# Six staging tiles for the outputs of a down projection, packed operands, and the order of two weight loads in a decoder step

## The chip, the core and the metric

The kernel runs on one core of a Trainium2 chip. The metric is the device time of one execution in microseconds (us); lower is better. The kernel's median over 3 runs is 1246.54 us (1244.26 to 1247.14). Line numbers (L303) are those of the kernel before, unless a row is said to be of the changed one, where most lines are one less or more.

## The reference

One step of a decoder layer for 512 prompt tokens and 8 x 4 sample tokens (544 columns in all), D_MODEL 1024, D_FF 2816. Two token mixers (a gated convolution and a sparse attention) are merged, then comes the part that the change works on:

```
x  = x + g1 * (merged @ w_out)
h2 = rmsnorm(x, norm2) * (1 + sc2) + sh2
x  = x + g2 * ((silu(h2 @ w_gate) * (h2 @ w_up)) @ w_down)
y  = rmsnorm(x, norm_f)
```

All of it is fp32.

## The kernel before

**Arithmetic.** Every fp32 operand is split into a high and a low part (`to_hilo`: ACT rounds the high part, L396, DVE subtracts for the low part, L397), and a product is three matmuls (`mm3`): high x high (L254), high x low (L255), low x high (L256), each 128 x 128 by 272 columns in the part spoken of here. Results gather in PSUM.

**The FFN.** The 22 chunks of 128 hidden features are worked in pairs c2 = 1 to 10; chunks 0 and 1 are done ahead, by plain products (the loop over `early`, whose gate tiles `ffg` lie in a pool of their own, `wx`). The hidden dimension is cut into four phases for the down projection, of 4, 6, 6 and 6 chunks. A pair of output tiles is computed by `seven`, a scheme with seven block products in place of eight: `wpair` is a generator that issues the seven products of one pair, `product` their matmuls into the PSUM tiles wA, wB and wC, and `snap` (L303, ACT) copies an intermediate sum of wA into a quarter of the tile `work`. Between them DVE adds a snap to the PSUM tile of the next result and writes the output (`out`). The last two products of a pair (`rest`) are held back and issued in the middle of the next pair. A pair takes a slab of weights (`slab`, L240, requested by SP, from a ring of three buffers `raw`) and, for its block sums, a second, partly summed tile `ws` (L318, SP too, two buffers); DVE completes these by two additions (L359, L364), and ACT and DVE split them.

`combine` makes the sums of the input h2 that the scheme multiplies with: t0 to t3, four `tf` tiles in the pool `f6`, split into T1 to T4 in hooks that run during the first pairs.

**Phases.** Phase 0 is `down_plain`, run during c2 = 2: eight outputs m by plain products. `gated` (ACT L1835, and DVE L1838 for the sample columns) scales the result by g2 from PSUM into a staging tile of 128 x 544, and `add_x1` (L1841) has POOL start a DMA that adds the staging tile onto x in DRAM (`x_dr<-work`, 272 KB). Four staging tiles are used in turn: the two halves of `U` and of `Gs[1]`. Phases 1 and 2 are `down_seven`, run during c2 = 5 and c2 = 8 between the gate and the up product: four pairs dn0 to dn3 of two outputs. `dn_out` adds a snap into the staging tile (DVE L1863), scales it in place, and `add_x1` sends it when its second half is there. The first result of a pair goes to its first tile, the second one to the second tile, `rest` completes the second tile and then the first:

```
for m2, ts in enumerate(((u0, u1), (v0, v1), (u1, u0), (v1, v0))):
```

u0, u1 are the halves of `U`, v0, v1 those of `Gs[ph - 1]`. So dn2 first writes u1, which dn0 completed first. Phase 3 ends the kernel with plain products and the final norm.

**Memory.** `work` holds Gs[0], Gs[1], U and the four snaps; each gate product writes Gs[c2 % 2] (L1767), each up product writes U (L1779, L1814) and multiplies. A tile that is written again waits for its readers, the DMA out to DRAM among them. [...]

Of the kernel before, what the change touches and what calls it, by code (L numbers as in the profile page):

```python
# [10 lines left out]
F32 = mybir.dt.float32  # L11
# [12 lines left out]
NT = TP + TS  # L24
# [134 lines left out]
def build(tc, a, o):  # L159
# [30 lines left out]
    def nm(s):  # L190
        uid[0] += 1
        return f"{s}_{uid[0]}"
# [93 lines left out]
    def seven(o_, ww, wlp, wsp):  # L286
        wi, ns, late = [0], [0], [iter(())]
        hooks = iter(o_.splits)

        def wsplit(view, odd=None):  # L290
            nk = view.shape[1]
            if odd is None:
                wi[0] += 1
                odd = wi[0] % 2
            pools = ((wpool, "wh"), (wpool, "wl")) if odd else ((ww, "Wh"), (wlp, "Wl"))
            wh, wl = (p_.tile([128, 8, 128], F32R, tag=t, bufs=2, name=nm(t))[:, 0:nk, :] for p_, t in pools)
            to_hilo(view, wh, wl)
            return wh, wl

        def snap(p):  # L300
            t = o_.snaps[ns[0] % 4]
            ns[0] += 1
            o_.snap_ops.append(act.activation(t, p, AF.Copy))  # L303
            return t

        def product(p, w, k0, X, first):
            n_ = len(X[0]) if isinstance(X[0], list) else 4
            xk = lambda t, k: t[k] if isinstance(t, list) else t[:, k, :]
            k0 *= n_
            for k in range(n_):  # L310
                mm3(p, w[0][:, k0:k0 + n_], w[1][:, k0:k0 + n_], xk(X[0], k), xk(X[1], k), k, first and k == 0, k == n_ - 1, skip_group_check=not first)

        def wslab(*key):
            raw = slab(*key)
            n_ = len(SLABS[key][1]) // 4
            if key in pre:
                t = wsp.tile([128, 16, 128], F32, tag="ws", bufs=2, name=nm("ws"))
                sync.dma_start(t[:, n_:3 * n_].rearrange("p k f -> p (k f)"), pre[key][:, 0:256 * n_])  # L318
                y, z = t[:, 0:2 * n_], t[:, 2 * n_:4 * n_]
            else:  # L320
                y, z = (wsp.tile([128, 8, 128], F32, tag="ws", bufs=3, name=nm("ws"))[:, 0:2 * n_] for _ in range(2))
            q = raw.rearrange("p k f -> p (k f)").rearrange("p (n k f) -> p n k f", n=4, k=n_)
            return q, y, z, key in pre

        def prepare(slabs):

            raw, y, z, summed = slabs
            n_ = raw.shape[2]
            y1, y2, z1, z2 = y[:, 0:n_], y[:, n_:2 * n_], z[:, 0:n_], z[:, n_:2 * n_]
            a22, a21, a11, a12 = (raw[:, i] for i in range(4))  # L330
            W0 = wsplit(raw[:, 2:4].rearrange("p n k f -> p (n k) f"))
            if not summed:
                dve.tensor_add(y2, a21, a22)
            dve.tensor_add(y1, y2, a11)
            WY = wsplit(y)
            if not summed:
                dve.tensor_add(z1, a11, a21)
            dve.tensor_add(z2, y1, a12)
            return W0, WY

        def wpair(slabs, out, ready=None, o_=o_, tie=None):

            raw, y, z, summed = slabs
            n_ = raw.shape[2]
            y1, y2, z1, z2 = y[:, 0:n_], y[:, n_:2 * n_], z[:, 0:n_], z[:, n_:2 * n_]
            a22, a21, a11, a12 = (raw[:, i] for i in range(4))
            W0 = wsplit(raw[:, 2:4].rearrange("p n k f -> p (n k) f")) if ready is None else ready[0]
            pA = s_ps(nm("wA"))[:, 0:WH]
            product(pA, W0, 0, o_.B11, True)
            s1 = snap(pA)  # L350
            pB = lin_ps(nm("wB"))[:, 0:WH]
            product(pB, W0, 1, o_.B21, True)
            out(0, 0, pB, s1)
            yield
            if ready is None:
                if not summed:
                    dve.tensor_add(y2, a21, a22)
                with tc.issue_after(tie.ins) if tie else ExitStack():
                    dve.tensor_add(y1, y2, a11)  # L359
                WY = wsplit(y)  # L360
                if not summed:
                    dve.tensor_add(z1, a11, a21)
                with tc.issue_after(tie.ins) if tie else ExitStack():
                    dve.tensor_add(z2, y1, a12)  # L364
            else:
                WY = ready[1]
            WZ = wsplit(z)
            W3 = wsplit(a22)
            product(pA, WY, 0, o_.T2, False)
            s2 = snap(pA)  # L370
            next(hooks, lambda: None)()
            pC = lin_ps(nm("wC"))[:, 0:WH]
            product(pC, WY, 1, o_.T1, True)
            next(late[0], None)
            next(hooks, lambda: None)()
            product(pA, WZ, 0, o_.T3, False)
            s3 = snap(pA)
            out(1, 1, pC, s3)
            next(hooks, lambda: None)()

            def rest():
                product(pA, W3, 0, o_.T4, False)
                out(1, 0, pA, None)
                yield
                product(pC, WZ, 1, o_.B22, False)
                out(0, 1, pC, s2)
                yield
            late[0] = rest()
            yield
        return SimpleNamespace(wsplit=wsplit, wslab=wslab, wpair=wpair, late=late, prepare=prepare)  # L390
# [1307 lines left out]
    def combine():  # L1698

        fq = lambda k, q: h2f[:, kq[k], Q[q]]  # L1700
        t0, t1 = (f6_tile(i, [128, 4, WH], F32, "tf") for i in (6, 7))
        t2, t3 = (f6_tile(i, [128, 4, WH], F32, "tf") for i in (3, 2))
        act.activation(t2, fq(0, 1), AF.Copy, scale=-1.0)
        pool.dma_start(t2, fq(1, 1), accum_op=ALU.add)
        dve.tensor_sub(t0, fq(0, 0), fq(0, 1))
        act.activation(t3, fq(1, 0), AF.Copy)
        dve.scalar_tensor_tensor(t1, t0, -1.0, fq(1, 1), ALU.mult, ALU.subtract)
        pool.dma_start(t3, t1, accum_op=ALU.add)
        to_hilo(t1, *T2)

        def split_t3():
            with tc.issue_after(snap_ops[1].ins):
                to_hilo(t2, *T3)

        def split_t4():
            with tc.issue_after(snap_ops[1].ins):
                act.activation(T4[0], t3, AF.Copy, scale=-1.0)
                dve.scalar_tensor_tensor(T4[1], t3, -1.0, T4[0].bitcast(F32), ALU.mult, ALU.subtract)
        return [lambda: to_hilo(t0, *T1), split_t3, split_t4]

    early = []
    wxst = ExitStack()
    wx = mkpool(wxst, "wx", side="right")
    for c in range(2):
        cs = slice(c * 128, c * 128 + 128)
        w = [split(v[:, :, cs]) if c == 0 else tuple(f6_tile(2 + 2 * n_ + j, [128, 8, 128], F32R, "wx") for j in range(2)) for n_, v in enumerate((sg, su))]
        if c:
            with tc.issue_after(n2_ops[0][0].ins), tc.issue_after(n2_ops[0][1].ins):
                to_hilo(sg[:, :, cs], *w[0])
        ffn_tiles(c)  # L1730
        early.append((c, wx.tile([128, NT], F32, name=nm("ffg")), w))
    for hf in range(2):
        for c, g_, w in early[::1 - 2 * hf]:
            ffn_gate(g_, w[0], hf)
# [6 lines left out]
                    to_hilo(su[:, :, 128:256], *early[1][2][1])  # L1741
        if hf == 0:
            ops_.splits = combine()
    wxst.close()
    n2st.close()
    work = wk.tile([128, KC * NT], F32, tag="work", bufs=1, name="work")
    cut = lambda i, n: work[:, i * WH:(i + n) * WH]
# [44 lines left out]
    def up_seven(G, c2):  # L1792
        if c2 % 3 == 2:
            tt = [f_x[:, 4 * i:4 * i + 4] for i in range(2)]
            bb = [f_x[:, 8 + i] for i in range(6)]
        else:
            tiles = [f6_tile(4 * (c2 % 3 == 0) + i, [128, 4, WH], F32R, "fs") for i in range(4)]
            tt = tiles[0:2]
            bb = [tiles[2 + i // 4][:, i % 4] for i in range(6)]
        ops = fops.setdefault((c2 - 2) // 3, {n: ([], []) for n in ("B11", "B21", "B22", "T1", "T2", "T3", "T4")})  # L1800
        for n, i in (("B11", 0), ("B21", 2), ("B22", 4)):
            for x in range(2):
# [40 lines left out]
    def down_plain():  # L1843

        nk = PHASES[0][1]
        stg = [t[:, m, :] for t in (U, Gs[1]) for m in range(2)]
        for m in range(KC):
            if m % 2 == 0:
                sl_ = slab("dn", 0, m // 2)
            w = split(sl_[:, :, (m % 2) * 128:(m % 2) * 128 + 128], nk=nk)  # L1850
            t = stg[m % 4]
            for hf in range(2):
                p = lin_ps(nm("dn"))[:, 0:HW[hf]]
                for k in range(nk):
# [14 lines left out]

    def down_seven(ph):  # L1870
        o_ = SimpleNamespace(**fops[ph - 1])
        u0, u1, v0, v1 = (t[:, m, :] for t in (U, Gs[ph - 1]) for m in range(2))
        for m2, ts in enumerate(((u0, u1), (v0, v1), (u1, u0), (v1, v0))):
            yield wslab("dn", ph, m2), dn_out(m2, ts), o_

    def finish_pair():
# [193 lines left out]
```

## Time and profile before

| | |
|---|---|
| median of 3 runs | 1246.54 us |
| the profiled execution | 1244.05 us, its span 1242.3 us |
| mean granted TensorE clock | 0.994 |
| PE busy, of the 840 us up to the FFN's pairs | 828.56 us |
| PE busy, of the 402.3 us after that | 380.73 us |
| copies of staging tiles to DRAM | 24, of 272 KB, median 7.5 us to landing |

A row of the timeline has the start, the length, the engine and line, the operation, what it writes and reads, and in brackets the idle time of the engine just before and what ended it. Rows of the stretches give length, busy time (and count) for PE, PE's weight loads, DVE, ACT and POOL, the granted clock (1.00 is full), the share of the DMA engines, and GB/s.

### The profile page before, as it was taken

Reading aid. Unit: us, or ns where it says so; the run is one execution under the profiler, and the core shown is the slowest. Engines: PE = TensorE matmul, PEld = TensorE weight load, DVE = VectorE, ACT = ScalarE, POOL = GpSimd, SP = SyncE. Lnnn points to the kernel's source line nnn. Section 1 sums busy time; section 2 is a strip of 40 time slices with the busy share of each in tenths; the row PEclk is TensorE's granted clock in tenths of the full one; section 3 lists DMA queues with packets and bytes.
Section 4 is the critical chain, followed back from the end, with each engine's and each line's share of the span. In section 5 each row is a group of like instructions: output and inputs, shape, how many; then the busy total and the mean of one; then the engine's idle time right before and its main releaser. Section 6 shows DMA issues by size and latency. Waiting matters only on the chain.

```text
span 1242.3 us, 25810 instructions
## 1 busy us (share of the span) xinstructions
PE 1209.3 (97%) x10158; PEld 1113.3 (90%) x10158; DVE 845.0 (68%) x1891; ACT 673.5 (54%) x1323; POOL 100.1 (8%) x154
## 2 busy tenths in 40 slices
PE   8999999999999999999999999999999998998997
PEld 6998999999999888787777779999899998998997
DVE  4467646887775576686776866758747856876766
ACT  5556535664445333386766664437555655665542
POOL 1000210000000111120100100000020011001000
PEclk9999999999999999999999999999999999999999
DMA  8953238787674998979787878716385366447612
GB/s 283 407 201 139 90 131 215 234 247 215 206 207 150 367 329 299 313 211 247 212 232 213 235 225 267 269 64 175 109 224 171 119 188 205 151 138 213 205 52 73
DMA packets 83660, 255.65 MB, mean 206 GB/s; under 512 B 9160, under 2 KB 19272, under 8 KB 69338
## 3 DMA queue, kind: packets, MB, share of 16 engines
q1 hardware_dynamic: 70994, 230.51, 53.3%
q0 software_dynamic: 12112, 23.09, 11.4%
q8 instruction: 80, 1.31, 0.4%
q10 hardware_dynamic: 432, 0.39, 0.1%
q14 instruction: 42, 0.34, 0.1%
HBM read 223.15 MB, written 65.28 MB: 232 GB/s over the span
## 4 chain that ended last, share of the span: by engine, by line
PE 41%; issue 9%; DMA 4%; DVE 3%; ACT 2%; POOL 1%; DVEq 0%; ACTq 0%; POOLq 0%
PE lin L255 5%; PE lin L254 4%; PE lin L256 4%; PE acc L1477 3%; PE ptp L1483 3%; PE wA L254 2%; PE wA L256 2%; PE wA L255 2%; PE modp L415 1%; PE dn L256 1%; PE dn L254 1%; DMA x_dr<-work 1%; PE dn L255 1%; DMA raw<-in_wt 1%; PE sp L1449 1%
## 5 line engine op out<-in xcount | busy, mean ns | idle before, releaser
L254 PE MATMUL lin<-h_h,wh 128*128 128x288 f32 (+1 forms) x352 | 103.9, 295 | 0.0
L255 PE MATMUL lin<-h_l,wh 128*128 128x288 f32 (+1 forms) x352 | 101.7, 289 | 0.0
L256 PE MATMUL lin<-h_h,wl 128*128 128x288 f32 (+1 forms) x352 | 101.3, 288 | 0.0
L303 ACT ACTIVATE work<-wA 128x272 f32<-128x272 f32 x141 | 55.3, 393 | 73.8 <-PE wA L256 70.9
L397 DVE TENSOR_TENSOR Wl<-ws,Wh 128x1024 fp32r<-128x1024 f32 (+1 forms) x47 | 55.4, 1179 | 40.1 <-ACT Wh L396 38.9
L250 DVE TENSOR_TENSOR wl<-raw,wh 128x1024 fp32r<-128x1024 f32 (+1 forms) x50 | 56.8, 1136 | 34.0 <-ACT wh L249 33.5
L249 ACT ACTIVATE wh<-raw 128x1024 fp32r<-128x1024 f32 (+1 forms) x50 | 49.3, 986 | 52.4 <-PE lin L255 31.4
L1456 ACT ACTIVATE P<-P,nms 128x384 f32<-128x384 f32 (+3 forms) x120 | 65.0, 543 | 20.1 <-DVE nms L1455 19.4
L685 PE MATMUL phi<-xh,wph 128*128 128x256 f32 x256 | 72.2, 290 | 2.1 <-ACT wph L593 1.6
L254 PEld LDWEIGHTS lin<-h_h,wh 128*128 128x128 f32 x352 | 66.8, 190 | 7.7 <-issue 6.2
L1455 DVE CUSTOM_DVE_ANT_0 P<-sp,ta 128x384 f32<-128x384 f32 (+3 forms) x120 | 52.1, 468 | 30.1 <-PE sp L1443 22.7
L685 PE MATMUL phi<-xl,wph 128*128 128x256 f32 x256 | 70.5, 284 | 1.5 <-DVE xl L668 1.5
L685 PE MATMUL phi<-xh,wpl 128*128 128x256 f32 x256 | 70.2, 283 | 0.0
L255 PEld LDWEIGHTS lin<-h_l,wh 128*128 128x128 f32 x352 | 66.4, 189 | 0.1
L256 PEld LDWEIGHTS lin<-h_h,wl 128*128 128x128 f32 x352 | 66.1, 188 | 0.1
L397 DVE TENSOR_TENSOR wl<-ws,wh 128x1024 fp32r<-128x1024 f32 (+1 forms) x47 | 55.3, 1178 | 13.8 <-ACT wh L396 13.1
L396 ACT ACTIVATE Wh<-ws 128x1024 fp32r<-128x1024 f32 (+1 forms) x47 | 48.0, 1021 | 28.6 <-PE wC L255 26.2
L396 ACT ACTIVATE wh<-raw 128x1024 fp32r<-128x1024 f32 (+2 forms) x51 | 51.0, 1001 | 22.6 <-PE wC L255 14.2
L396 ACT ACTIVATE wh<-ws 128x1024 fp32r<-128x1024 f32 (+1 forms) x47 | 48.1, 1024 | 27.7 <-PE wB L255 24.4
L397 DVE TENSOR_TENSOR wl<-raw,wh 128x1024 fp32r<-128x1024 f32 (+2 forms) x51 | 58.6, 1149 | 2.0 <-ACT wh L396 2.0
L558 POOL DMA_DIRECT2D pre<-in_wt x28 | 27.2, 972 | 370.7 <-DMA pre<-in_wt 370.7
L685 PEld LDWEIGHTS phi<-xh,wph 128*128 128x128 f32 x256 | 47.5, 189 | 4.0 <-ACT wph L593 1.8
(600 smaller groups left out, 4435.9 us busy)
## 6 DMA issues: line engine op xcount, KB each, us to landing
raw<-in_wt SPq DMA_DIRECT2D x89, 1024.0 KB, 6.6
sraw<-in_cache_sel SPq DMA_DIRECT2D x64, 256.0 KB, 5.1
gt<-in_cache_cmp SPq DMA_DIRECT2D x56, 256.0 KB, 5.5
pre<-in_wt SPq DMA_DIRECT2D x20, 512.0 KB, 9.2
pre<-in_wt POOLq DMA_DIRECT2D x20, 512.0 KB, 7.6
ws<-pre SPq DMA_DIRECT2D x20, 512.0 KB, 3.4
raw<-in_wt SPq DMA_DIRECT2D x12, 768.0 KB, 5.2
wraw<-in_cache_winT SPq DMA_DIRECT2D x8, 1024.0 KB, 8.8
```

The costliest lines, as they stand in the source:

```text
L249: act.activation(oh, view, AF.Copy)
L250: dve.tensor_sub(ol, view, oh.bitcast(F32))
L254: pe.matmul(p, lhsT=wh[:, k, :], rhs=xh, start=start, stop=False, **kw)
L255: pe.matmul(p, lhsT=wh[:, k, :], rhs=xl, start=False, stop=False, **kw)
L256: pe.matmul(p, lhsT=wl[:, k, :], rhs=xh, start=False, stop=stop, **kw)
L303: o_.snap_ops.append(act.activation(t, p, AF.Copy))
L396: act.activation(hi, src, AF.Copy)
L397: return dve.tensor_sub(lo, src, hi.bitcast(F32))
L685: pe.matmul(po[:, s * 256:s * 256 + 256], lhsT=w, rhs=m, start=(n_ == 0), stop=(n_ == len(ops) - 1))
L1455: p_ops.append(dve.tensor_tensor_reduce(out=t[:, 0:n], in0=sps[br], in1=t_dist[:, 512 - n:512], scale=-hs, scalar=3e38, op0=ALU.add, op1=A ...
L1456: e_ops.append(act.activation(t[:, 0:n], t[:, 0:n], AF.Exp, scale=-1.0, bias=nms[:, c:c + 1], accum_out=sums[:, c:c + 1]))
L1477: pe.matmul(acc[br * 64:br * 64 + 64, :], lhsT=vtok[br][:, j, g * 64:(g + 1) * 64], rhs=pts_[br], start=(j == 0), stop=False)
```

## The change

It has six parts.

1. In `wslab` the partly summed tile `ws` is requested before the slab `raw`.
2. t0 and t1 of `combine` lie in the memory of x1, which is free once x is in DRAM.
3. The gate tiles of chunks 0 and 1 lie in a new tile `dsp` (128 x 2 x 544) of the pool `f6`; the pool `wx` is gone. `dsp` stays as two more staging tiles.
4. The operands that `up_seven` keeps for `down_seven` take three tiles and a half-size one, in place of four tiles.
5. `down_plain` uses six staging tiles in turn: U, Gs[1] and dsp.
6. `down_seven` has six staging tiles: dn2 writes s0 and u1, dn3 writes s1 and v1 (s0, s1 are the halves of dsp).

```
         def wslab(*key):
-            raw = slab(*key)
             n_ = len(SLABS[key][1]) // 4
             if key in pre:
                 t = wsp.tile([128, 16, 128], F32, tag="ws", bufs=2, name=nm("ws"))
...
+            raw = slab(*key)
...
-        t0, t1 = (f6_tile(i, [128, 4, WH], F32, "tf") for i in (6, 7))
+        tx = x1_slot("tf", F32, WH)
+        t0, t1 = tx[:, 0:4], tx[:, 4:8]
...
-    wxst = ExitStack()
-    wx = mkpool(wxst, "wx", side="right")
+    dsp = f6.tile([128, 2, NT], F32, tag="dsp", bufs=1, name="dsp")
...
-        early.append((c, wx.tile([128, NT], F32, name=nm("ffg")), w))
+        early.append((c, dsp[:, c, :], w))
...
-    wxst.close()
...
-            tiles = [f6_tile(4 * (c2 % 3 == 0) + i, [128, 4, WH], F32R, "fs") for i in range(4)]
-            tt = tiles[0:2]
-            bb = [tiles[2 + i // 4][:, i % 4] for i in range(6)]
+            late_ = c2 % 3 == 0
+            tt = [f6_tile(3 * late_ + i, [128, 4, WH], F32R, "fs") for i in range(2)]
+            bb = [t[:, i] for t in (f6_tile(3 * late_ + 2, [128, 4, WH], F32R, "fs"), f6.tile([128, 2, WH], F32R, tag=f"fg{late_:d}", bufs=1, name=nm("fs"))) for i in range(t.shape[1])]
...
-        stg = [t[:, m, :] for t in (U, Gs[1]) for m in range(2)]
+        stg = [t[:, m, :] for t in (U, Gs[1], dsp) for m in range(2)]
...
-            t = stg[m % 4]
+            t = stg[m % 6]
...
-        u0, u1, v0, v1 = (t[:, m, :] for t in (U, Gs[ph - 1]) for m in range(2))
-        for m2, ts in enumerate(((u0, u1), (v0, v1), (u1, u0), (v1, v0))):
+        u0, u1, v0, v1, s0, s1 = (t[:, m, :] for t in (U, Gs[ph - 1], dsp) for m in range(2))
+        for m2, ts in enumerate(((u0, u1), (v0, v1), (s0, u1), (s1, v1))):
```

How this stands on the engines is shown at three places.

First, DVE in phase 1, where the first result of dn2 is written (the addition from wB), before:

```order
L364 TENSOR_TENSOR ws_13060<-ws_13060,raw_13058 128x384
L1863 TENSOR_TENSOR work<-wB_12975,work 128x272
L1838 TENSOR_TENSOR work<-work,modT 128x32
L397 TENSOR_TENSOR wl_13007<-ws_12958,wh_13006 128x768
L397 TENSOR_TENSOR Wl_13011<-raw_12956,Wh_13010 128x384
```

and now:

```order
L364 TENSOR_TENSOR ws_13052<-ws_13052,raw_13054 128x384
L1862 TENSOR_TENSOR dsp<-wB_12969,work 128x272
L1837 TENSOR_TENSOR dsp<-dsp,modT 128x32
L397 TENSOR_TENSOR wl_13001<-ws_12950,wh_13000 128x768
L397 TENSOR_TENSOR Wl_13005<-raw_12952,Wh_13004 128x384
```

The order is the same; the addition and its scaling go to `dsp` in place of a half of `U`, with the splits of the next weights behind them as before.

Second, DVE at the end of `down_plain` (the additions L1838 are those of the outputs 4 to 7) and the start of the up product of c2 = 2 (L1814), before:

```order
L1838 TENSOR_TENSOR work<-dn_11881,modT 128x32
L397 TENSOR_TENSOR Wl_12062<-raw_12015,Wh_12061 128x512
L250 TENSOR_TENSOR wl_11948<-raw_11945,wh_11947 128x512
L1838 TENSOR_TENSOR work<-dn_11915,modT 128x32
L359 TENSOR_TENSOR ws_12110<-ws_12110,raw_12108 128x512
L250 TENSOR_TENSOR wl_11982<-raw_11945,wh_11981 128x512
L364 TENSOR_TENSOR ws_12110<-ws_12110,raw_12108 128x512
L1838 TENSOR_TENSOR work<-dn_11951,modT 128x32
L397 TENSOR_TENSOR wl_12020<-raw_12015,wh_12019 128x1024
L1838 TENSOR_TENSOR work<-dn_11985,modT 128x32
L397 TENSOR_TENSOR wl_12058<-ws_12017,wh_12057 128x1024
L1814 TENSOR_TENSOR work<-wB_12037,work 128x272
```

and now:

```order
L1837 TENSOR_TENSOR dsp<-dn_11875,modT 128x32
L397 TENSOR_TENSOR Wl_12056<-raw_12011,Wh_12055 128x512
L250 TENSOR_TENSOR wl_11942<-raw_11939,wh_11941 128x512
L1837 TENSOR_TENSOR dsp<-dn_11909,modT 128x32
L359 TENSOR_TENSOR ws_12102<-ws_12102,raw_12104 128x512
L250 TENSOR_TENSOR wl_11976<-raw_11939,wh_11975 128x512
L364 TENSOR_TENSOR ws_12102<-ws_12102,raw_12104 128x512
L1837 TENSOR_TENSOR work<-dn_11945,modT 128x32
L397 TENSOR_TENSOR wl_12014<-raw_12011,wh_12013 128x1024
L1837 TENSOR_TENSOR work<-dn_11979,modT 128x32
L397 TENSOR_TENSOR wl_12052<-ws_12009,wh_12051 128x1024
L1813 TENSOR_TENSOR work<-wB_12031,work 128x272
```

Outputs 4 and 5 moved to `dsp`, outputs 6 and 7 are in `U`, which the addition L1814 (now L1813) writes next.

Third, SP where the weights of the first pairs are asked for (`x_dr<-x` are the copies of x to DRAM), before:

```order
L1626 DMA x_dr_111<-x_9824 128x544
L1626 DMA x_dr_112<-x_9824 128x544
L240 DMA raw_11404<-in_wt 128x2048
L240 DMA raw_11585<-in_wt 128x2048
L1570 DMA out_new_win_sample<-in_cache_win 64x2048
L318 DMA ws_11368<-pre_2924 128x1024
L318 DMA ws_11406<-pre_3216 128x1024
L318 DMA ws_11587<-pre_3487 128x1024
```

and now:

```order
L1626 DMA x_dr_111<-x_9824 128x544
L317 DMA ws_11360<-pre_2924 128x1024
L1626 DMA x_dr_112<-x_9824 128x544
L317 DMA ws_11398<-pre_3216 128x1024
L240 DMA raw_11400<-in_wt 128x2048
L240 DMA raw_11581<-in_wt 128x2048
L1570 DMA out_new_win_sample<-in_cache_win 64x2048
L317 DMA ws_11579<-pre_3487 128x1024
```

The first two sums stand ahead of the slabs; the third one, which needs a buffer that the first pair frees, stands where it stood.

## The prediction

> **What bounds the kernel now.** I read the busy shares first, then stretches of 10 us, then the lists of waits, then single rows.
>
> ```profile
> span 1242.3 us, 25810 instructions
> PE 1209.3 (97%) x10158; PEld 1113.3 (90%) x10158; DVE 845.0 (68%) x1891; ACT 673.5 (54%) x1323; POOL 100.1 (8%) x154
> ```
>
> PE is busy for 97% of the span and the change leaves its 10158 matmuls alone. So only time in which PE stands, or runs at a lower clock, can be won. Where the change works (from about 840 us), stretches of 10 us show where that is. The columns are: length, busy time and count of PE, PEld, DVE, ACT, POOL, granted clock, DMA share, GB/s.
>
> ```profile
> 870.00:880.00 10.00, 7.65 (x57) 6.99 (x56) 8.54 (x12) 6.81 (x10) 0.00 (x0) 1.00 0.29 105
> ...
> 1000.00:1010.00 10.00, 9.98 (x80) 9.77 (x80) 6.19 (x13) 7.12 (x14) 1.72 (x2) 1.00 0.59 169
> 1010.00:1020.00 10.00, 8.03 (x52) 7.79 (x51) 5.70 (x11) 4.52 (x10) 1.72 (x2) 0.83 0.57 177
> 1020.00:1030.00 10.00, 8.13 (x62) 7.59 (x60) 4.62 (x9) 5.58 (x11) 0.86 (x1) 1.00 0.81 220
> 1040.00:1050.00 10.00, 8.17 (x65) 7.95 (x64) 4.91 (x10) 3.23 (x7) 0.56 (x1) 1.00 0.66 173
> 1050.00:1060.00 10.00, 9.96 (x67) 9.96 (x68) 9.09 (x17) 6.82 (x12) 0.00 (x0) 0.83 0.40 159
> 1120.00:1130.00 10.00, 9.43 (x70) 8.60 (x68) 4.58 (x9) 4.61 (x10) 1.72 (x2) 1.00 0.87 254
> 1130.00:1140.00 10.00, 7.36 (x47) 7.36 (x48) 6.42 (x11) 5.61 (x11) 1.72 (x2) 0.83 0.74 208
> ```
>
> An undisturbed stretch holds 80 matmuls (1000 to 1010), 8 per us. Every matmul short of 80 is 0.125 us of lost time, whether PE stood or its clock was down. That is my measure of loss below. Who is waited for there, in the lists of waits between 840 and 1200 us of PE and between 860 and 1160 us of DVE (total, times, longest):
>
> ```profile
> PE wA L254 <- ACT work L303: 9.1, 7, 2.7
> ```
> ```profile
> DVE work L1863 <- DMA x_dr<-work: 12.6, 3, 5.2
> DVE work L1767 <- DMA x_dr<-work: 5.1, 1, 5.1
> DVE work L1863 <- PE wC L255: 4.9, 1, 4.9
> ```
>
> PE waits for a snap (L303, ACT); ACT and DVE wait further back. DVE waits for `x_dr<-work`, the copy of a staging tile out to DRAM: the next pair's result is written into a tile whose copy has not landed. The rows of DVE in phase 1 and 2, and of POOL, which starts the copies:
>
> ```profile
> 1013.56 0.44 DVE L1863 TENSOR_TENSOR work<-wB,work 128x272 f32<-128x272 f32 x1 [4.92 <-PE wC L255]
> 1024.65 0.44 DVE L1863 TENSOR_TENSOR work<-wB,work 128x272 f32<-128x272 f32 x1 [4.46 <-DMA x_dr<-work]
> 1047.32 0.44 DVE L1767 TENSOR_TENSOR work<-wB,work 128x272 f32<-128x272 f32 x1 [5.09 <-DMA x_dr<-work]
> 1130.57 0.44 DVE L1863 TENSOR_TENSOR work<-wB,work 128x272 f32<-128x272 f32 x1 [5.24 <-DMA x_dr<-work]
> ```
> ```profile
> 1004.04 0.86 POOL L1841 DMA_DIRECT2D x_dr<-work  x1 [75.10 <-DVE work L1838]
> 1015.96 0.86 POOL L1841 DMA_DIRECT2D x_dr<-work  x1 [7.76 <-DVE work L1838]
> 1036.64 0.86 POOL L1841 DMA_DIRECT2D x_dr<-work  x1 [5.71 <-DVE work L1838]
> 1121.06 0.86 POOL L1841 DMA_DIRECT2D x_dr<-work  x1 [5.75 <-DVE work L1838]
> ```
>
> Paired in order these give the time from a copy's start to the write that waited for it: 1013.56 - 1004.04 = 9.5, then 8.7, 10.7 and 9.5 us. The first is put down to PE in its row, but it is the copy of `u1` too: the pair dn2 writes `u1` first. The rows of PE at the first of these places, and the stretches around two of them:
>
> ```profile
> 1013.36 0.29 PE L256 MATMUL wC<-fs,wl 128*128 128x272 f32 x1
> 1015.63 0.39 PE L254 MATMUL wA<-f_x,wh 128*128 128x272 f32 x1 [1.97 <-ACT work L303]
> ```
> ```profile
> 1016.30:1019.70 3.40, 3.40 (x17) 3.39 (x16) 3.33 (x6) 1.61 (x5) 1.37 (x2) 0.50 0.93 357
> 1050.50:1054.00 3.50, 3.50 (x18) 3.50 (x17) 3.03 (x4) 1.78 (x3) 0.00 (x0) 0.52 0.62 242
> 1129.60:1132.60 3.00, 0.33 (x3) 0.11 (x1) 2.00 (x5) 1.56 (x5) 0.00 (x0) 0.96 0.31 55
> 1132.60:1135.80 3.20, 3.16 (x14) 3.16 (x15) 2.31 (x4) 2.50 (x4) 0.86 (x1) 0.50 0.78 271
> ```
>
> After a stall of 2.3 us start to start (1013.36 to 1015.63), and one of 3.0 us, a stretch at clock 0.50 to 0.52 follows: 17, 18 and 14 matmuls where 8 per us would give 27, 28 and 26. Three such stretches cost (10 + 10 + 12) x 0.125 = 4.0 us, already in the 10 us counts.
>
> **The change part by part.** No matmul, addition, split or transfer is added or removed, so each term is a wait.
>
> *Six tiles in `down_seven`* (dn2 and dn3 write into `dsp` first, not into `u1` and `v1`). Removed are the four waits above and the smaller ones at dn2 of phase 2. Phase 1: (80 - 52) + (80 - 62) + (80 - 65) + (80 - 67) = 74 matmuls, 74 x 0.125 = 9.2 us. Phase 2: (80 - 70) + (80 - 47) = 43 matmuls, 5.4 us. What is late next, first the gate after the pairs. It writes `v0` first (1047.32), which dn3 no longer touches, and `v1`, whose copy is now the one of 1036.64, with a later addition:
>
> ```profile
> 1054.23 0.43 DVE L1767 TENSOR_TENSOR work<-wC,work 128x272 f32<-128x272 f32 x1
> ```
>
> That is 6.9 us after the first one. Without the wait both come 5.1 us earlier, `v1` at 1049.1, against 1036.64 + 10.7 = 1047.3: clear by 1.8 us. `u1` is written again in dn2, but by the same later addition of the pair; a down pair multiplies over three blocks of 128 in each product where a gate has four, so I estimate 6.9 x 0.75 = 5.2 us after the first addition, which comes at the earliest at 1013.56 - 4.92 = 1008.6. So `u1` is written at 1013.8 or later against 1013.56: just clear, and a copy slower by 1.2 us costs about 1 us. The pairs dn0 and dn1 ran without a wait at full pace (80 matmuls in 1000 to 1010), so splits, snaps and additions keep up. I take both sums whole; if the loads hold a pair up, a part comes back (a rival below).
>
> *Six tiles in `down_plain`.* No DVE wait on a copy in phase 0 is in the list, so nothing is won there. But output 6 now lands in the first tile of `U` (before, output 4 did, and 6 went to `Gs[1]`), and the next up product writes that tile.
>
> ```profile
> 924.61 0.86 POOL L1841 DMA_DIRECT2D x_dr<-work  x1 [3.41 <-DMA out_new_win_sample<-in_cache_win]
> ```
> ```profile
> 929.56 0.44 DVE L1814 TENSOR_TENSOR work<-wB,work 128x272 f32<-128x272 f32 x1 [0.88 <-PE wB L256]
> 930.47 1.23 DVE L397 TENSOR_TENSOR wl<-raw,wh 128x1024 fp32r<-128x1024 f32 x1 [0.47 <-ACT wh L396]
> ```
> ```profile
> 934.09 0.29 PE L256 MATMUL wA<-h_hi,wl 128*128 128x272 f32 x1
> ```
> ```profile
> x_dr<-work POOLq DMA_DIRECT2D x24, 272.0 KB, 7.5
> ```
>
> This is a new wait: the addition at 929.56 must wait for the copy of 924.61. Queued behind it on DVE is the split of 930.47, whose result PE reads at 934.09. Addition and split take 0.44 + 1.23 = 1.67 us, so the copy may take 934.09 - 924.61 - 1.67 = 7.8 us before PE stands. Nearest rows: the median of 24 copies is 7.5 us (no cost), the longest wait above 10.7 (2.9 us, and a slow stretch of 1.3 us behind it). Below nothing it cannot go. I take 0.3 us: this copy has the light traffic of phase 0, so I stay by the median.
>
> *Weight sums asked for ahead, gate tiles out of their own pool.* At the start of the pairs PE waits for splits of a pre-summed tile, which are late because the additions into it are late:
>
> ```profile
> 873.01 0.40 PE L254 MATMUL wA<-T_hi,wh 128*128 128x272 f32 x1 [0.92 <-ACT wh L396]
> 874.88 0.40 PE L256 MATMUL wA<-T_hi,wl 128*128 128x272 f32 x1 [1.10 <-DVE wl L397]
> ```
> ```profile
> 869.52 0.68 DVE L359 TENSOR_TENSOR ws<-ws,raw 128x512 f32<-128x512 f32 x1
> ```
> ```profile
> SPq L318 <- DVE f_hilo L397: 16.2, 1, 16.2
> ```
>
> SP stood 16.2 us before it could ask for the second pair's sums, since their buffer shared memory with the gate tiles. Now both requests stand ahead of the raw slabs and the additions ahead of the first snaps. In all, 870 to 880 loses (80 - 57) x 0.125 = 2.9 us. I take the two waits that name the splits, 0.92 + 1.10 = 2.0 us. The rest I leave: the third sum's addition still stands in DVE's queue ahead of splits and waits for a buffer that the first pair frees. Ends: 0 and 2.9 us. On SP the later requests already alternate (a sum, then the next pair's slab), so nothing else moves there.
>
> *Packed operands, `tf` in the place of x1.* These free memory; same instructions, nothing. The first write of `tf` now waits for the copies of x to DRAM, which SP starts near 840 us, long before it is needed near 854.
>
> Sum: 9.2 + 5.4 + 2.0 - 0.3 = 16.3 us. On the profiled execution, 1244.05 (span 1242.3 and 1.75 around it), this gives 1227.75. The median of the runs is 1246.54, 2.5 higher: 1230.2, my number.
>
> The page's row on the clock: 0.50 follows idle stretches of 2.3 and 3.0 us here. [...]
>
> The copies' rows say 7.5 us and more. [...]
>
> **The rivals.**
>
> *The slow stretches stay.* PE still has short stalls, and the clock may drop all the same. For it: the first stretch came after only 2.3 us. Against it: undisturbed pairs show no stall. Gain 16.3 - 4.0 = 12.3, time 1234.2. Chance 0.13.
>
> *The small terms turn bad.* The copy into `U` takes 10.7 us: 4.2 in place of 0.3, and the start wins nothing: 16.3 - 3.9 - 2.0 = 10.4, time 1236.1; one alone gives 1232 to 1234. Chance 0.10.
>
> *Another wait comes in its place.* Without the copies' wait, the next late thing (a sum or slab from DRAM) keeps half of the time: gain 8, time 1238. For it: DMA is 0.81 to 0.87 busy in 1020 to 1030 and 1120 to 1130. Against: dn0 to dn1. Chance 0.04.
>
> *The change does not do what it says.* If PE was held by something that ends at the same time as the copies, nothing moves: 1244 to 1248. Against it stands that one row of DVE each names the copy. Chance 0.03.
>
> *Slower: the loads become the bound of the down pairs.* One pair needs these:
>
> ```profile
> raw<-in_wt SPq DMA_DIRECT2D x12, 768.0 KB, 5.2
> ws<-pre SPq DMA_DIRECT2D x8, 384.0 KB, 2.9
> ```
>
> With two copies of 272 KB that is 1.7 MB in a pair of 8.0 us, 210 GB/s. To undo 16.3 us and go over 2.5 us beyond, each of 8 pairs would have to lose 2.4 us, so take 10.4 us: that decides from under 163 GB/s. The rows show 254 over 10 us and 357 over 3.4 us. It would give 1249 and over. Chance 0.03.
>
> **How the numbers follow.** The forecast (gain 13 to 19.5) has the rest, 0.67. 1230.2 is its time. The range takes its ends, 1227 to 1233.5, goes up to 1236 for the first two rivals and down to 1226 for a start that wins all and for runs that scatter: 1226 to 1236. About 0.2% (2.5 us) is what a measurement of this kernel can tell from no change. Faster by more: 0.67 + 0.13 + 0.10 + 0.04 = 0.94; within it 0.03; slower 0.03.
>
> **What would show it.** In the profile after: no DVE wait on `x_dr<-work` of over 1 us in the two phases; 78 to 80 matmuls in each 10 us there; no stretch at clock 0.50 between the pairs; near 870 to 880 fewer than 10 matmuls missing; one new DVE wait at the first L1813 addition of the up product after phase 0, of 2.5 us or a little more, with PE short by under 1 us. I am wrong if waits of 4 to 5 us on other transfers stand where the copies' were, or if PE slows without a stall.

## The result and the profile after

The changed kernel takes 1227.64 us in the median of 6 runs (1227.24 to 1229.79), the kernel before 1246.84 us (6 runs, 1244.26 to 1250.4). The ratio is 0.9847, with a 95% interval of 0.9831 to 0.9863. The profiled execution took 1227.63 us (span 1225.8); that of before took 1244.05 us, so the two traces differ by 16.4 us and the medians by 19.2.

The page of the changed kernel:

```profile
span 1225.8 us, 25813 instructions
PE 1204.2 (98%) x10158; PEld 1109.9 (91%) x10158; DVE 844.9 (69%) x1891; ACT 675.4 (55%) x1323; POOL 100.2 (8%) x154
```

The same 10158 matmuls, and the same work on DVE, ACT and POOL within 2 us. What is gone is time in which PE stood or ran slowly. The stretches of 10 us of the changed kernel, with the columns as before:

```profile
870.00:880.00 10.00, 9.56 (x75) 9.31 (x75) 7.70 (x11) 5.91 (x9) 0.00 (x0) 1.00 0.32 105
...
1010.00:1020.00 10.00, 10.00 (x80) 9.80 (x79) 6.34 (x13) 6.99 (x14) 2.58 (x3) 1.00 0.94 272
1020.00:1030.00 10.00, 10.00 (x80) 9.85 (x80) 6.85 (x11) 6.47 (x12) 1.72 (x2) 1.00 0.81 227
1040.00:1050.00 10.00, 10.00 (x80) 9.79 (x79) 9.73 (x17) 6.26 (x13) 0.00 (x0) 1.00 0.42 154
1120.00:1130.00 10.00, 10.00 (x81) 9.95 (x79) 7.08 (x11) 6.54 (x12) 1.72 (x2) 1.00 0.85 249
1130.00:1140.00 10.00, 10.00 (x80) 9.86 (x79) 7.54 (x14) 5.45 (x9) 0.86 (x1) 1.00 0.83 218
```

Every stretch of the two phases holds 79 to 81 matmuls at clock 1.00, also where before 47 to 70 stood. The DMA engines move more in the same time (272 GB/s in 1010 to 1020, 177 before) and this holds nobody up. PE's waits between 840 and 1200 us and DVE's waits for copies between 860 and 1160 us, in the changed kernel:

```profile
PE dn L256 <- DVE wl L250: 1.3, 1, 1.3
PE wA L256 <- DVE wl L397: 0.4, 1, 0.4
PE wA L256 <- DVE Wl L397: 0.4, 1, 0.4
PE wA L254 <- ACT work L303: 0.4, 1, 0.4
```
```profile
DVE work L1813 <- DMA x_dr<-work: 4.4, 1, 4.4
```

PE's wait for snaps fell from 9.1 to 0.4 us. Of DVE's waits for copies one is left, and it is new: the first tile of `U`, behind output 6 of `down_plain`. Its rows:

```profile
923.24 0.86 POOL L1840 DMA_DIRECT2D x_dr<-work  x1 [3.62 <-DVE work L1837]
```
```profile
931.70 0.44 DVE L1813 TENSOR_TENSOR work<-wB,work 128x272 f32<-128x272 f32 x1 [4.38 <-DMA x_dr<-work]
932.06 1.22 DVE L397 TENSOR_TENSOR wl<-raw,wh 128x1024 fp32r<-128x1024 f32 x1
```
```profile
933.33 0.39 PE L256 MATMUL wA<-h_hi,wl 128*128 128x272 f32 x1 [0.45 <-DVE wl L397]
```

The copy took 8.5 us to the addition that waited for it, the split behind the addition was late, and PE stood for 0.45 us.

### The profile page after: what moved, and what is told of

The parts are those of the page before. It is cut to its first block, busy times and chain, and to the rows that moved or that the text cites. A ratio compares the mean times of both kernels' runs of the same rounds, so it can differ in the third digit from the quotient of the medians.

```text
span 1225.8 us, 25813 instructions
## 1 busy us (share of the span) xinstructions
PE 1204.2 (98%) x10158; PEld 1109.9 (91%) x10158; DVE 844.9 (69%) x1891; ACT 675.4 (55%) x1323; POOL 100.2 (8%) x154
## 4 chain that ended last, share of the span: by engine, by line
PE 52%; DMA 2%; DVE 2%; ACT 1%; issue 0%; DVEq 0%; ACTq 0%
PE lin L255 5%; PE lin L254 5%; PE lin L256 5%; PE wA L254 4%; PE wA L256 4%; PE wA L255 4%; PE acc L1477 3%; PE ptp L1483 3%; PE wC L255 2%; PE wC L256 2%; PE wC L254 2%; DMA raw<-in_wt 2%; PE modp L415 1%; PE sp L1449 1%; PE dn L254 1%; PE dn L256 1%
```

## The experiments

Each kernel is the changed kernel with the edit shown, if nothing else is said. The times are medians. The kernel before ran beside each group of kernels: with a median of 1247.57 us beside the old targets, the old order of requests, the four tiles and the six tiles in another order; 1246.28 beside the kernel before once more, the memory alone and the two kernels with idle time; 1246.34 beside the memory without `dsp` and the sum put off; 1244.98 beside the gate tiles back in `wx` and the old targets once more.

**The old targets.**

```
-        for m2, ts in enumerate(((u0, u1), (v0, v1), (s0, u1), (s1, v1))):
+        for m2, ts in enumerate(((u0, u1), (v0, v1), (u1, u0), (v1, v0))):
```

> The changed kernel with one part undone: the targets of the down pairs are (u0, u1), (v0, v1), (u1, u0), (v1, v0) again. My theory (the waits for the copies of staging tiles carry most of the gain): it loses the 14.6 us of the two phases again, so about 1242 to 1245 us median, with three stretches at clock 0.50; and its runs scatter by several us, since each wait ends when a copy lands. Rival (the earlier sums and the memory carry more than their 2 us): it loses clearly less than 14 us, and its runs lie as close together as those of the changed kernel (within 1 us or so).

Measured: 1239.85 us (12 runs, 1238.02 to 1247.9), ratio to before 0.9943 (0.9922 to 0.9963). DVE's waits for copies in its trace:

```profile
DVE work L1862 <- DMA x_dr<-work: 15.1, 4, 5.1
DVE work L1766 <- DMA x_dr<-work: 7.8, 2, 5.5
DVE work L1813 <- DMA x_dr<-work: 7.7, 2, 5.0
DVE work L1784 <- DMA x_dr<-work: 2.7, 1, 2.7
```

The waits are back with this one line, and 12.2 us with them. That is less than the 14.6 expected and more than any other single undoing cost. The runs scatter over 10 us (12 runs), those of the changed kernel over 2.6 (6 runs), as my theory had it. Its number is missed on the low side (1242 to 1245 were expected), and of three slow stretches one came in the phases (from 1132 us; the clock was 0.67 in 1131.12 to 1134.12). The 12.2 us are less than the rival's 14 too, but with its close runs it fits worse. The rest of the gain, between this kernel and before, had to be looked for elsewhere.

**The old order of requests.**

```
         def wslab(*key):
+            raw = slab(*key)
             n_ = len(SLABS[key][1]) // 4
...
-            raw = slab(*key)
```

> The changed kernel with one part undone: the slab is requested before its partly summed tile. My theory: the two stalls near 872 and 875 us come back, 2.0 us, so 1229.6 us, and the rest of the trace is unchanged. Rival (the gate tiles in a tile of their own do it, since the second sum no longer waits for their memory): under 0.5 us lost. Other rival (the request order matters through the whole part): 4 us or more lost.

Measured: 1227.19 us (5 runs, 1226.14 to 1228.44). Nothing is lost, and the start is that of the changed kernel:

```profile
870.00:880.00 10.00, 9.60 (x77) 9.38 (x76) 7.89 (x9) 6.10 (x10) 0.00 (x0) 1.00 0.35 112
```

My theory falls here: the swapped requests give nothing. Of the rivals the first one holds, that the memory does it.

**Four tiles in `down_plain`.**

```
-            t = stg[m % 6]
+            t = stg[m % 4]
```

> The changed kernel with one part undone: down_plain uses four staging tiles in turn again (U and Gs[1]). My theory: the new DVE wait of 4.4 us at the first addition of the next up product goes, and with it 0.3 to 0.6 us of PE's time, so 1227.1 us. Rival (six tiles in phase 0 do win something elsewhere): it is slower by 0.5 us or more.

**The six tiles in another order.**

```
-        stg = [t[:, m, :] for t in (U, Gs[1], dsp) for m in range(2)]
+        stg = [t[:, m, :] for t in (dsp, U, Gs[1]) for m in range(2)]
```

> The changed kernel with the six tiles of down_plain in another order: dsp, U, Gs[1], so that outputs 6 and 7 lie in dsp and U is free early. My theory: no DVE wait on a copy at the first addition of the next up product; 0.3 to 0.6 us faster than the changed kernel, 1227.1 us, as with four tiles. Rival: the wait was covered by the later stalls, no difference (within 0.2 us).

Measured: 1228.74 us (1227.6 to 1230.12) and 1227.18 us (1226.63 to 1227.98), 5 runs each. The wait for the copy is gone in both traces, and the time is the changed kernel's within the scatter. The stall of 0.45 us was paid again a little later, by a stall at 937 us (0.3 and 0.55 us), behind a DVE wait for a sum from DRAM (4.8 and 5.0 us, 1.4 in the changed kernel). So the new wait costs nothing that can be measured, as the rival of the second of these two kernels said. Whether six tiles win something in phase 0, the rival of the first one, stays open: by the medians four tiles are 1.1 us slower, by the ratios to before (0.9849 and 0.9847) 0.2 us.

**The kernel before once more**, with no edit.

> The kernel before once more, for a second trace of it. With the old targets in the changed kernel 12.2 us were lost in the median, so 7.7 us lie between that kernel and the one before, where the first trace of before gives only some 2.4 us (the start). Theory A: the rest is in the copies' waits, which end when copies land, so that this trace shows waits of another length than the first trace of before (1013.56, 1024.65, 1047.32, 1118.66, 1130.57), in sum several us longer, while everything outside of the two phases and the start agrees within 1 us. Rival B: something before 840 us or after 1160 us is slower in most runs of before; then the time to 840 us or the end differs by several us. Time 1245 to 1249 us.

Measured: 1245.93 us (10 runs, 1243.0 to 1249.06); the profiled execution took 1245.96. Where phase 1 begins this trace agrees with the first one within 1 us (the first copy starts at 1003.40 and at 1004.04), but in phase 2 it differs:

```profile
1120.00:1130.00 10.00, 8.21 (x61) 7.55 (x60) 5.54 (x11) 5.47 (x11) 1.72 (x2) 1.00 0.77 237
1130.00:1140.00 10.00, 6.77 (x40) 6.33 (x39) 6.42 (x11) 4.76 (x9) 1.72 (x2) 0.83 0.71 205
```

Here 61 + 40 matmuls stand where the first trace had 70 + 47: 16 less, 2.0 us, as much as the two executions differ (1.9). The first copy of phase 2 took 8.7 us to land in this one and 7.4 in the first. So the waits, and with them the time, change from execution to execution of the same program, as theory A had it, though by 2 us and not by the 5 us or so that it had to find. The first wait of dn2, which the first trace put down to PE, is put down to the copy here:

```profile
1013.16 0.44 DVE L1863 TENSOR_TENSOR work<-wB,work 128x272 f32<-128x272 f32 x1 [5.17 <-DMA x_dr<-work]
```

**The memory alone**: the old targets, the old order of requests and four tiles in `down_plain`, with the three edits shown above. Only `dsp` for the gate tiles, `tf` in the place of x1 and the packed operands are left of the change.

> The changed kernel with request order, down_plain and the targets undone, so that only the memory differs from before (gate tiles in dsp, tf in the place of x1, packed operands). The order of requests by itself cost nothing in the changed kernel, so by the theory that the gate tiles' own memory gives the start (2 to 2.5 us) this lies with the kernel with the old targets, 1239 to 1241 us, and the start shows one stall of some 0.6 us instead of three. Rival (the request order matters as long as copies are waited for): it lies near before, 1244 to 1247 us.

Measured: 1240.47 us (12 runs, 1237.39 to 1245.21), ratio to before 0.9955 (0.9937 to 0.9972), so 5.6 us faster than before by the ratio. The start has 77 matmuls in 870 to 880:

```profile
870.00:880.00 10.00, 9.66 (x77) 9.44 (x76) 7.28 (x10) 6.17 (x9) 0.00 (x0) 1.00 0.35 116
```

The start is won by memory alone, and the order of requests does not matter beside the copies' waits either.

**Memory without `dsp`.** The kernel before with two parts alone, `tf` in the place of x1 and the packed operands; the gate tiles stay in `wx`.

```
-        t0, t1 = (f6_tile(i, [128, 4, WH], F32, "tf") for i in (6, 7))
+        tx = x1_slot("tf", F32, WH)
+        t0, t1 = tx[:, 0:4], tx[:, 4:8]
...
-            tiles = [f6_tile(4 * (c2 % 3 == 0) + i, [128, 4, WH], F32R, "fs") for i in range(4)]
-            tt = tiles[0:2]
-            bb = [tiles[2 + i // 4][:, i % 4] for i in range(6)]
+            late_ = c2 % 3 == 0
+            tt = [f6_tile(3 * late_ + i, [128, 4, WH], F32R, "fs") for i in range(2)]
+            bb = [t[:, i] for t in (f6_tile(3 * late_ + 2, [128, 4, WH], F32R, "fs"), f6.tile([128, 2, WH], F32R, tag=f"fg{late_:d}", bufs=1, name=nm("fs"))) for i in range(t.shape[1])]
```

> The kernel before with two parts of the change alone: tf in the place of x1, and the packed operands; the gate tiles stay in their own pool, and there is no dsp. The memory that this frees lets the first requests of partly summed tiles stand early in SP's order here too. Theory A (what helps at the start is that the sums' buffers share no memory with something in use, however that comes about): the start shows one stall of some 0.6 us in place of three, and the time is that of the kernel with the memory parts only, 1239 to 1242 us. Rival B (it takes the gate tiles in dsp): the three stalls and 1245 to 1247 us.

Measured: 1241.38 us (9 runs, 1238.85 to 1245.21), ratio 0.9961 (0.9944 to 0.9979); one stall of 0.4 us at the start, 76 matmuls in 870 to 880. Theory A: what helps is that the sums' buffers share no memory with something in use, and any memory does.

**The gate tiles back in `wx`**, with the rest of the change, the swapped requests among it.

```
     dsp = f6.tile([128, 2, NT], F32, tag="dsp", bufs=1, name="dsp")
+    wxst = ExitStack()
+    wx = mkpool(wxst, "wx", side="right")
...
-        early.append((c, dsp[:, c, :], w))
+        early.append((c, wx.tile([128, NT], F32, name=nm("ffg")), w))
...
+    wxst.close()
```

> The changed kernel with one part undone: the gate tiles of chunks 0 and 1 lie in their own pool wx again, whose memory the buffers of the sums take over; dsp serves as staging alone. No copy is waited for in the two phases, so this prices the start by itself. Theory A (the memory parts gave 5.8 us in the median, of which the start is 2.5 and the rest is the copies' waits, which are shorter there): the three stalls of 871 to 880 us come back and nothing else, 1230.1 us. Rival B (the start is worth the whole 5.8 us, by what it moves later): 1233 us.

Measured: 1230.36 us (6 runs, 1227.89 to 1233.8), 2.7 us over the changed kernel by the medians and 4.4 by the ratios to before beside each (0.9882, 0.9859 to 0.9904). The start is that of before, stall for stall, although `wslab` asks for the sum first:

```profile
870.00:880.00 10.00, 7.66 (x57) 7.00 (x56) 8.13 (x11) 7.17 (x11) 0.00 (x0) 1.00 0.31 105
```
```profile
PE wA L256 <- DVE wl L397: 1.1, 1, 1.1
PE wA L254 <- ACT wh L396: 0.9, 1, 0.9
PE wA L254 <- ACT Wh L396: 0.3, 1, 0.3
```
```profile
848.95 17.90 SPq L317 DMA_DIRECT2D ws<-pre  x2
866.52 8.79 SPq L317 DMA_DIRECT2D ws<-pre  x2
```

These rows of SP's queue (each for two requests in a row, from the start of the first to the end of the last; the second one of the first row is the first one of the second) say that the second sum is asked for at 866.5 us again, and the first at 848.95, behind the slabs. In the kernel with the old order of requests both stand at 840 to 841 us, ahead of them, although its `wslab` asks for the slab first:

```profile
840.15 0.32 SPq L318 DMA_DIRECT2D ws<-pre  x1
...
841.09 0.38 SPq L318 DMA_DIRECT2D ws<-pre  x1
844.04 3.42 SPq L240 DMA_DIRECT2D raw<-in_wt  x2
```

So in these kernels a free buffer sets the place of these requests, and not the order in the code. Theory A has the median; the interval does not exclude that the start is worth 4 us.

**The old targets once more**, for a second trace.

> The changed kernel with the old targets once more, for a second trace. The first copy of phase 1 took 9.4 and 9.6 us to land in the two traces of before, 6.7 to 7.0 in the traces with the memory changed. Theory A (that is a property of the program): 6.5 to 7.1 us again, and the first wait of dn2 is 2.0 to 2.6 us. Rival B (it differs by the execution): 8.5 us or more, and a first wait of over 4 us. Time 1238 to 1248 us.

Measured: 1245.64 us, one run. Neither number came: the first copy of phase 1 took 7.7 us and the wait was 3.25 us. With 6.7 in the first trace of the same program and 7.7 in this one, landings differ by the execution (rival B in kind). Why they came to 9.4 and 9.6 us in the two traces of before, the runs do not tell; a first copy of 8.8 and 9.3 us stands in the two kernels with idle time below, which have the memory of the changed kernel. The time of this one run says little of the old targets: ahead of the phases it holds a stall of 4.14 us between two matmuls (1.29 in the first trace), with a slow stretch behind it (clock 0.59 in 926.22 to 929.22).

```profile
925.62 0.40 PE L256 MATMUL dn<-f_hilo,wl 128*128 128x288 f32 x1 [3.85 <-DVE wl L250]
```

The stretch 920 to 930 holds 38 matmuls here and 73 in the first trace; 15 of the 35 come back up to 950, and 20 x 0.125 = 2.5 us are lost.

**Idle time put in on purpose**, two kernels.

```
+    STALL = {(1, 1): 4, (1, 3): 7, (2, 1): 10, (2, 3): 13}
...
                 dve.tensor_add(t[:, c], p, s_)
+                if (m, q) == (0, 0):
+                    for _ in range(STALL.get((ph, m2), 0)):
+                        dve.tensor_scalar_mul(t[:, c], t[:, c], 1.0)
```

The second one has 9, 12, 5 and 3 in these places.

> The changed kernel with idle time put in on purpose: after the first addition of the down pairs dn1 and dn3 the sum is multiplied by 1 in place, 4 and 7 times in phase 1, 10 and 13 times in phase 2 (some 0.35 us each on DVE), and ACT's scaling and the next snap wait for that. So PE gets four stalls of different length, estimated at 0 to 4 us. Theory (a stall of 2 us or more brings a stretch at half clock): each stall of 2.0 us or more is followed within 1 us by a stretch at clock 0.50, three and more us long, and no stall of under 1.7 us is. [...] Time 1228 to 1242 us.

> As the kernel before it, with 9 and 12 multiplications in phase 1 and 5 and 3 in phase 2. [...] Time 1228 to 1242 us.

Measured: 1229.3 and 1230.63 us, one run each. The stalls came out too short: the longest distance between two matmuls in the two phases was 1.27 us, since a multiplication took 0.3 us and splits ran between them. None of them was followed by a slow stretch, which fits the theory and does not test it. What tests it are stalls that nobody had planned, in all the traces (below).

**A sum put off**, together with the order dsp, U, Gs[1]: the additions of the gate pair c2 = 3 are tied behind the last split of `down_plain`.

```
-        gate = wpair(wslab("fg", c2), gate_out(G), tie=last_mod[0] if c2 == 1 else None)
+        gate = wpair(wslab("fg", c2), gate_out(G), tie=last_mod[0] if c2 == 1 else sub_op[0] if c2 == 3 else None)
```

`sub_op` holds the last subtraction that `split` issued.

> The changed kernel with two more edits: the six tiles of down_plain in the order dsp, U, Gs[1], and the additions into the sum of the gate pair c2 = 3 put behind the last split of down_plain, since DVE waited 3.9 us there for a slab with that split behind it, and PE 1.3 us for the split. My theory: the stall at 920 us goes, and 1.0 to 1.5 us with it, 1226.2 us in the median. Rival (the time is given back at the stall of 944 us, where the next pair waits for its sum from DRAM anyway): no difference beyond 0.3 us.

Measured: 1227.09 us (5 runs, 1224.67 to 1228.47), no clear difference. The stall at 920 us (1.08 us with the order dsp, U, Gs[1] alone) is gone and came back at 936 us. In this kernel L361 is the addition into the sum, L399 the split:

```profile
935.70 0.69 DVE L361 TENSOR_TENSOR ws<-ws,raw 128x512 f32<-128x512 f32 x1 [5.95 <-DMA ws<-pre]
```
```profile
938.30 0.39 PE L258 MATMUL wA<-T_hi,Wl 128*128 128x272 f32 x1 [1.49 <-DVE Wl L399]
```

DVE got there earlier and waited longer, 5.95 us in place of 5.00 with that order alone and 1.41 in the changed kernel, for a sum whose landing nobody moved; PE's stall behind it is 1.49 us in place of 0.55. So 0.94 of the 1.08 us came back, as the rival said, if earlier than at its 944 us. The median is that of the kernel with that order alone (1227.18) within the scatter.

## Why the prediction was right, and where it was not

**The copies' waits (14.6 us) were the gain.** Every stretch with missing matmuls is full, the three slow stretches are gone, and the old targets alone bring 12.2 us back. The starts of the same copies, from POOL's rows, show where the time went:

| us | before | before, second trace | changed |
|---|---|---|---|
| first copy of phase 1 | 1004.04 | 1003.40 | 1002.60 |
| first copy of phase 2 | 1111.18 | 1110.83 | 1100.39 |
| end of the span | 1242.3 | 1244.1 | 1225.8 |

Between the first two rows the changed kernel gains 9.4 us on the first trace, and from there to the end 5.7, where 9.2 and 5.4 were predicted. On the second trace it gains 9.6 and 7.9, in sum 17.5.

That undoing gives 2 us less than 14.6 has a reason that I did not settle: the first copy landed 1.7 to 2.9 us earlier in both traces with the old targets than in both of before. Nor do the parts undone one at a time add up: the old targets (12.2) and the gate tiles back in `wx` (2.7, by the ratios 4.4) make 14.9 to 16.4 of the 19.2 us. The rest shows only where both are undone, as in the kernel before, and its cause is open.

**The slow stretches went with the stalls.** The rival (the clock drops all the same, 1234.2) fell: no stretch is below 1.00 in the phases.

**The new wait on `U` (0.3 us) came** at its place, with 4.4 us on DVE against some 2.5 predicted, since this copy took 8.5 us and not the median of 7.5; PE paid 0.45 us. The reason given for the median, light traffic in phase 0, was a misreading. In the trace of before the DMA engines were busy all through this copy, and the same copy took 8.4 us there:

```profile
924.60:932.20 7.60, 7.60 (x63) 7.60 (x62) 3.71 (x5) 3.75 (x6) 1.72 (x2) 1.00 1.04 324
x_dr<-work POOLq DMA_DIRECT2D x1, 272.0 KB, 8.4
```

That is over the 7.8 us from which PE stands, so this row gave 0.6 us; the 0.3 came near by luck. Taking the wait away wins nothing that can be measured.

**The start (2.0 us) had the right size and, for one half, the wrong reason.** It gained (75 - 57) x 0.125 = 2.3 us in the trace, 2.7 us by undoing it alone (4.4 by the ratios). But I named two causes, the memory shared with the gate tiles and the requests ahead of the slabs. Undoing the second costs nothing, undoing the first brings back all three stalls with the second in place. The third sum's addition stayed behind as foreseen, as one stall of 0.4 us.

**The step that failed is the last one**, from the profiled execution to the median: "The median of the runs is 1246.54, 2.5 higher: 1230.2". The sum of 16.3 us hit the difference of the two traces (16.4), but 1230.2 is 2.6 us above the measured 1227.64. I treated the 2.5 us as something that stays. The second trace of before says that they went with the waits: at 1245.96 us it lies near the median, and its phases are worth 17.5 us. With these in place of 14.6 the sum is 19.2, which is the difference of the medians. The first trace had caught short waits (15.1 by the same count), and the changed kernel's median is its profiled time. This rests on one more trace of before.

There is some luck in the 16.4 too. The changed kernel's trace was 0.8 us late when the copies of x began (841.01 against 840.22), ahead of what the change does. Three kernels that are the same up to there (the changed one, the old targets, the old order of requests) stand at 841.01, 842.26 and 838.55, so single traces differ by some us that no term of the sum is about.

The scatter fits. Kernels that wait for copies in the phases spread over 6 to 12 us (before 1241.97 to 1253.84 in one group of 23 runs and 1244.26 to 1250.4 in one of 6, 1238.02 to 1247.9 with the old targets, 1237.39 to 1245.21 with the memory alone). Those that do not, in 5 or 6 runs each, spread over 1.4 to 3.8 us, save that with the gate tiles in `wx` (5.9).

The range (1226 to 1236) held. The loads did not become the bound: 272 GB/s were moved in 1010 to 1020 where the pairs were reckoned to need 210.

## What to carry to other kernels

In the four waits of before a staging tile was written again 8.7 to 10.7 us after its copy was started, when the copy had landed: where a buffer is sent out by DMA, count the pairs between the issue and the next write, and price the worst landing in the trace, not the median. Where the waits vary with the landings, as here, the median can lie above a lucky trace (1246.84 against 1244.05 us), and that excess belongs to what the removal wins. Before a stall off the main path is mended, look at what is late next: the mends tried here moved a stall by 4 to 16 us and won nothing that could be measured. And read a trace's sum against more than one execution: here two traces of the same program differ by 2.4 us in the phases alone.

## What the runs showed of the hardware

**The clock behind a stall.** In the 14 traces, from 840 to 1200 us, 47 distances between the starts of two matmuls are over 1.0 us. None of the 28 up to 1.88 us was followed by a slow stretch. Of the 19 from 2.16 to 4.14 us, 16 were (a mean clock of 0.50 to 0.78 in the 3 us that begin 0.6 us behind the start of the next matmul), and three were not: 2.19, 2.42 and 2.62 us, with 1.00 in the same 3 us. So the theory of the kernels with idle time, a slow stretch behind each stall of 2.0 us or more, does not hold as it was stated. The stall of 2.62 us, in the kernel with the old targets, went on at clock 1.00:

```profile
1047.78 0.39 PE L254 MATMUL wA<-T_hi,wh 128*128 128x272 f32 x1 [2.33 <-ACT work L303]
```
```profile
1048.38:1051.38 3.00, 2.48 (x17) 1.92 (x15) 2.67 (x4) 1.64 (x3) 0.00 (x0) 1.00 0.75 292
```

The shorter one of 2.16 us, in the kernel before (1047.88 to 1050.04), went on at 0.50:

```profile
1050.64:1053.64 3.00, 3.00 (x15) 3.00 (x15) 2.67 (x4) 1.65 (x3) 0.00 (x0) 0.50 0.55 216
```

So the length of a stall alone did not settle it.

**Landings.** A copy of 272 KB that adds onto DRAM took 5.4 to 10.6 us to land in the two phases of the first trace of before, and 4.9 to 10.0 us in those of the changed kernel. The same copy of the same program differed by 1.0 and 1.3 us between two executions (6.7 and 7.7, 7.4 and 8.7).
